# A strided-slice copy whose transfers are issued under a limit of six per queue

## The chip, the cores and the metric

The kernel runs on one core of a Trainium2 chip. The metric is device time in microseconds (us), the median over repeated executions; lower is better. The kernel does no arithmetic: it only moves data, so the engines that matter are the two that issue transfers, SyncE (SP) and ScalarE (ACT), and the core's 16 DMA engines that carry them out.

## The reference

```python
batch, seq, dim = 32, 1024, 512          # float32
start, stop, stride = 0, 512, 2
def reference(x, start, stop, stride):
    return x[:, start:stop:stride, :].astype(np.float32)
```

Of each of the 32 batches every second row among the first 512 is kept: 256 rows of 512 floats, 2 KB each. The output has the shape (32, 256, 512), which is 16.78 MB, so 16.78 MB must be read from HBM and 16.78 MB written to it.

## The kernel before

Each batch's 256 kept rows are split by the parity of their place into two halves of 128 rows. `two(t, b, step, parity)` (line 16 and on) picks one such half of the two batches `b` and `b + step`: 128 x 2 rows of 2 KB, 512 KB. `apart(b)` says which parity of batch `b` goes which way. Every transfer in the kernel has this form, 256 pieces of 2 KB.

One half goes straight from HBM to HBM: 16 transfers, issued by ACT on line 40. The other half goes through on-chip memory: 16 loads into the tile `held`, issued by SP on line 39, and 16 stores out of it, issued on line 47, eight by SP and eight by ACT. So each of the two queues gets 24 transfers of 512 KB, and 25.17 MB are moved in all, since half of the data is moved twice. Below, the transfers of a queue are numbered from #0 to #23 in the order of their issue: SP's #0 to #15 are loads and #16 to #23 stores; ACT's #0 to #15 are direct copies and #16 to #23 stores.

The order is written out by hand, inside a section that the framework does not reorder. The first loop (lines 35 to 40) alternates a load on SP and a direct copy on ACT, for four groups of eight batches. The second loop (lines 41 to 47) goes over the groups again: both engines wait until the group's four loads have landed (lines 42 and 43, one semaphore `loaded` per group, 64 counts), and then issue the group's stores, SP for even and ACT for odd `b`. `held` has room for all batches, so no transfer waits for a buffer. At the end SP waits for all stores of its own and for everything that ACT issued (lines 48 and 49, the semaphores `done`). An engine issues its transfers in this order, each instruction behind the one before it; nothing in the code says how many transfers may be under way.

Of the kernel before, what the change touches and what calls it, by code (L numbers as in the profile page):

```python
# [3 lines left out]

EIGHT = 8


def apart(b):


    return 1 - (b >> 1 & 1)


def two(t, b, step, parity):

    return t[b : b + step + 1 : step].rearrange("b (p two) d -> two p b d", two=2)[parity]


def kernel(tc, x, start, stop, stride, out):

    nc = tc.nc
    src = x[:, start:stop:stride, :]
    B, rows, D = out.shape
    P = rows // 2
    sp, act = nc.sync, nc.scalar
    groups = range(0, B, EIGHT)
    with tc.tile_pool(name="io", bufs=1) as io:  # L30
        held = io.tile([P, B, D], x.dtype, name="held")
        with tc.tile_critical():
            loaded = [nc.alloc_semaphore(name=f"loaded{g}") for g in groups]
            done = [nc.alloc_semaphore(name=f"done{i}") for i in range(2)]
            for g in groups:
                for i, (b, step) in enumerate(((0, 5), (2, 5), (1, 3), (3, 3))):
                    b += g
                    at = g + 2 * i
                    sp.dma_start(held[:, at : at + 2], two(src, at, 1, 1 - apart(at))).then_inc(loaded[g // EIGHT], 16)
                    act.dma_start(two(out, b, step, apart(b)), two(src, b, step, apart(b))).then_inc(done[1], 16)  # L40
            for g in groups:
                for queue in (sp, act):
                    queue.wait_ge(loaded[g // EIGHT], 16 * 4)
                for b in range(g, g + 4):
                    k = b % 2
                    to = two(out, b, 4, 1 - apart(b))
                    (sp, act)[k].dma_start(to, held[:, b : b + 5 : 4]).then_inc(done[k], 16)
            sp.wait_ge(done[0], 16 * (B // 4))
            sp.wait_ge(done[1], 16 * (B // 2 + B // 4))


# [1 line left out]
_INS = ['x', 'start', 'stop', 'stride']  # L53
_OUTS = [((32, 256, 512), 'float32')]

_NUMBERS = {'start': 0, 'stop': 512, 'stride': 2}


def kernel(**inputs):
    import numpy as _np  # L60
    import concourse.bacc as _bacc
    import concourse.tile as _tile
    from concourse import mybir as _mybir
    from concourse.bass_utils import run_bass_kernel_spmd as _run

    nc = _bacc.Bacc("TRN2", target_bir_lowering=False, num_devices=1)  # L66
    arrays, args = {}, []
    for name in _INS:
        if name in _NUMBERS:
            args.append(_NUMBERS[name])  # L70
            continue
        a = _np.ascontiguousarray(inputs[name])
        if a.dtype.kind in "iu":
            a = a.astype(_np.int64)
        arrays[f"in_{name}_dram"] = a
        args.append(nc.dram_tensor(f"in_{name}_dram", a.shape, _mybir.dt.from_np(a.dtype), kind="ExternalInput").ap())
    for i, (shape, dtype) in enumerate(_OUTS):
        dt = _mybir.dt.from_np(_np.dtype(dtype))
        args.append(nc.dram_tensor(f"out_{i}_dram", shape, dt, kind="ExternalOutput").ap())
    with _tile.TileContext(nc) as tc:  # L80
        kernel(tc, *args)
    r = _run(nc, [arrays], core_ids=[0])
    got = tuple(r.results[0][f"out_{i}_dram"] for i in range(len(_OUTS)))
    return got[0]
```

## Time and profile before

| | |
|---|---|
| median of 5 runs | 81.22 us (81.00 to 82.00) |
| profiled execution, its own time | 82.17 us |
| span of its instructions | 80.4 us |
| outside the span | 1.8 us |
| moved by the DMA engines | 25.17 MB, mean 313 GB/s over the span |
| transfers, KB each, per queue | 24 of 512 KB on SP's queue, 24 on ACT's |
| median from issue to landing | 22.6 us (direct copies), 22.9 us (loads), 21.6 and 21.0 us (stores) |

No compute engine does anything but four tiny fills at the start. In the profile's table of slices, a digit is the mean busy share of the 16 DMA engines in tenths in one fortieth of the span (2.01 us), and the row under it is what they moved in GB/s. The two queues are named q1 and q10 there. An issue of a transfer is an instruction on SP or ACT (shown as SPq and ACTq); its duration is the time for which it holds its engine, not the time of the transfer. "To landing" is the time from the start of the issue to the last of the transfer's sixteen semaphore counts. In the profile's account by windows, the DMA share is the same busy share over a chosen stretch; as overlaps are counted, it can read slightly over 1. A "wait" of SPq is the time for which the engine stood at a semaphore.

### The profile page before, as it was taken

The numbers are of one execution on the slowest core, as the hardware profiler recorded it, in microseconds if no ns is written. First come the engines' busy times: TensorE is split into PE (matmuls) and PEld (weight loads), VectorE is DVE, ScalarE is ACT, GpSimd is POOL, SyncE is SP. The second block draws the span as 40 slices with busy tenths as digits, with TensorE's granted clock in tenths as the row PEclk, the third lists the DMA queues.
The fourth block names the chain that finished last, engine by engine and source line by source line (L and its number), as shares of the span: only waits on it lengthen the run. The fifth ranks groups of instructions, "written<-read, shape, count | busy, mean of one in ns | idle before, by whom it ended". The sixth has DMA issues, their size and how long they took to land. (4 is left out here: it accounts for less than half of the span.)

```text
span 80.4 us, 99 instructions
## 1 busy us (share of the span) xinstructions
POOL 0.2 (0%) x4
## 2 busy tenths in 40 slices
POOL 0000000000000000000000000000000000000000
DMA  0897699999999999999999999999999999999920
GB/s 0 267 306 214 175 328 378 373 334 373 357 281 400 378 305 314 302 295 224 356 374 348 350 367 324 319 335 408 409 406 367 349 347 352 356 353 360 342 94 8
DMA packets 13056, 25.17 MB, mean 313 GB/s; under 512 B 768, under 2 KB 768, under 8 KB 13056
## 3 DMA queue, kind: packets, MB, share of 16 engines
q1 hardware_dynamic: 6528, 12.58, 47.4%
q10 hardware_dynamic: 6528, 12.58, 46.9%
HBM read 16.78 MB, written 16.78 MB: 417 GB/s over the span
## 5 line engine op out<-in xcount | busy, mean ns | idle before, releaser
L66 POOL MEMSET const-bfloat16-1.0<- 128x1 bf16 x1 | 0.1, 101 | 0.0
L66 POOL MEMSET const-uint8-127<- 128x1 uint8 x1 | 0.1, 101 | 0.0
L66 POOL MEMSET const-float32-0.0<- 128x1 f32 x1 | 0.1, 98 | 0.2 <-issue 0.2
L66 POOL MEMSET const-float32-1.0<- 128x1 f32 x1 | 0.1, 98 | 0.0
## 6 DMA issues: line engine op xcount, KB each, us to landing
out_dram<-in_x_dram ACTq DMA_DIRECT2D x16, 512.0 KB, 22.6
held<-in_x_dram SPq DMA_DIRECT2D x16, 512.0 KB, 22.9
out_dram<-held SPq DMA_DIRECT2D x8, 512.0 KB, 21.6
out_dram<-held ACTq DMA_DIRECT2D x8, 512.0 KB, 21.0
```

Source lines behind the costliest of these rows:

```text
L66: nc = _bacc.Bacc("TRN2", target_bir_lowering=False, num_devices=1)
```

## The change

A helper class `Paced` takes the place of the plain issues, one object per queue. It numbers the queue's transfers, gives each two in a row a semaphore of their own (32 counts when both have landed), and before it issues the first of a new pair from the fourth pair on, it makes the issuing engine wait until the pair three before it has landed in full. So with #6 the engine waits for #0 and #1, with #8 for #2 and #3, and so on; at most six transfers of a queue are under way, and four just before a pair is issued. The transfers, their order on each queue, their shapes and what they move stay as they are. The waits for a group's loads become waits for two pairs (line 63 of the new kernel), and the final wait of SP goes over 16 semaphores (lines 66 to 68) where it was two.

```diff
+class Paced:
+    def __init__(self, nc, engine, name):
+        self.nc, self.engine, self.name = nc, engine, name
+        self.sems, self.n = [], 0
+
+    def start(self, to, frm):
+        if self.n % 2 == 0:
+            self.sems.append(self.nc.alloc_semaphore(name=f"{self.name}{self.n}"))
+            if len(self.sems) > 3:
+                self.engine.wait_ge(self.sems[-4], 32)
+        self.engine.dma_start(to, frm).then_inc(self.sems[-1], 16)
+        self.n += 1
+
+    def wait(self, on, first, last):
+        for sem in on.sems[first // 2 : last // 2]:
+            self.engine.wait_ge(sem, 32)
...
-            loaded = [nc.alloc_semaphore(name=f"loaded{g}") for g in groups]
-            done = [nc.alloc_semaphore(name=f"done{i}") for i in range(2)]
+            sp, act = Paced(nc, nc.sync, "sp"), Paced(nc, nc.scalar, "act")
...
-                    sp.dma_start(held[:, at : at + 2], two(src, at, 1, 1 - apart(at))).then_inc(loaded[g // EIGHT], 16)
-                    act.dma_start(two(out, b, step, apart(b)), two(src, b, step, apart(b))).then_inc(done[1], 16)
+                    sp.start(held[:, at : at + 2], two(src, at, 1, 1 - apart(at)))
+                    act.start(two(out, b, step, apart(b)), two(src, b, step, apart(b)))
             for g in groups:
                 for queue in (sp, act):
-                    queue.wait_ge(loaded[g // EIGHT], 16 * 4)
+                    queue.wait(sp, g // 2, g // 2 + 4)
                 for b in range(g, g + 4):
-                    k = b % 2
-                    to = two(out, b, 4, 1 - apart(b))
-                    (sp, act)[k].dma_start(to, held[:, b : b + 5 : 4]).then_inc(done[k], 16)
-            sp.wait_ge(done[0], 16 * (B // 4))
-            sp.wait_ge(done[1], 16 * (B // 2 + B // 4))
+                    (sp, act)[b % 2].start(two(out, b, 4, 1 - apart(b)), held[:, b : b + 5 : 4])
+            for queue in (sp, act):
+                sp.wait(queue, B // 2, queue.n)
+            sp.wait(act, 0, B // 2)
```

More of the change, by code (lines that the diff above doesn't have):

```diff
@@ L27 @@
     P = rows // 2
-    sp, act = nc.sync, nc.scalar
     groups = range(0, B, EIGHT)
```

## The prediction

> **What bounds the kernel now.** I read the slices of the page first, then the account by windows, then the issues in order of time, then SP's waits. The slices and the queues:
>
> ```profile
> DMA  0897699999999999999999999999999999999920
> GB/s 0 267 306 214 175 328 378 373 334 373 357 281 400 378 305 314 302 295 224 356 374 348 350 367 324 319 335 408 409 406 367 349 347 352 356 353 360 342 94 8
> q1 hardware_dynamic: 6528, 12.58, 47.4%
> q10 hardware_dynamic: 6528, 12.58, 46.9%
> ```
>
> The DMA engines are busy nearly throughout, 94.3% of 16 engines' span, so the time is set by how fast they move 25.17 MB. Two places are not at 9: the start (slices 2 to 6) and the tail (the last two). And a slice at 9 can still be slow: 281 and 224 GB/s are at 9 too; there the engines are busy but their packets take longer. I then cut the span where the rate changes. Columns are: stretch, its length, POOL's busy time, granted clock, DMA share, GB/s.
>
> ```profile
> 4.00:6.00 2.00, 0.00 (x0) 1.00 0.96 307
> 6.00:7.00 1.00, 0.00 (x0) 1.00 0.95 279
> 7.00:9.50 2.50, 0.00 (x0) 1.00 0.53 151
> 9.50:12.00 2.50, 0.00 (x0) 1.00 1.01 309
> 12.00:22.00 10.00, 0.00 (x0) 1.00 1.05 364
> ...
> 24.00:36.00 12.00, 0.00 (x0) 1.00 1.03 331
> 36.00:38.40 2.40, 0.00 (x0) 1.00 1.01 243
> 38.40:54.00 15.60, 0.00 (x0) 1.00 1.03 346
> 54.00:62.00 8.00, 0.00 (x0) 1.00 1.05 399
> 62.00:76.00 14.00, 0.00 (x0) 1.00 1.05 352
> ```
>
> The reader is to see one row: from 7.0 to 9.5 us the share is 0.53, that is, half of the engines stand idle, though by 7.0 us 14 transfers have been issued, two more are being issued and only one has landed. Everywhere later the share is about 1. So the only idle DMA time of any size between ramp and tail is here. What do the issuing engines do then?
>
> ```profile
> 5.98 2.43 SPq L39 DMA_DIRECT2D held<-in_x_dram  x1
> 6.75 6.66 ACTq L40 DMA_DIRECT2D out_dram<-in_x_dram  x1
> ...
> 8.45 0.93 SPq L39 DMA_DIRECT2D held<-in_x_dram  x1
> 9.42 7.75 SPq L39 DMA_DIRECT2D held<-in_x_dram  x1
> ```
>
> Columns: start, duration. The first issues take 0.43 to 1.05 us each; ACT's #7, at 6.75 us, is held for 6.66 us, SP's #7 for 2.43 and SP's #9 for 7.75. From then on most issues take 2.2 us or more: issue is stopped by what is under way. The first such stop and the half-idle stretch begin together. That is a coincidence in time and no proof of a cause.
>
> **How many are under way without the limit.** Each queue moves 24 transfers between about 2 and 79 us, one per 3.2 us. A median landing 22.6 us after issue makes 22.6 / 3.2 = 7 under way. So the change takes a natural depth of about seven to between four and six. This is the quantity to keep in mind: the steady state is hardly touched, the start is (by 9.4 us SP has issued nine and begun a tenth, ACT has finished seven and hangs in the eighth; paced, each stops at six).
>
> **The change part by part.**
>
> *The pacing waits* (nine on each queue). Behind each wait on SP and ACT stand only later transfers of the same queue and, on SP, the final wait; so a late refill costs only if the queue runs dry. When a pair is released, four transfers are left, 4 x 3.2 = 12.8 us of work. Against it stands the refill: a wait passed, two issues of about 0.5 us, and from issue to first bytes about 1.1 us (first issue at 0.91, packets from 2.0), 2.2 us together. Engines do not land together, so the lagging one counts: in the tail the stretch 77.2 to 78.8 us runs at 47 GB/s, an eighth of the full rate, so some engines are 1.6 us behind. 12.8 - 2.2 - 1.6 leaves 9 us of cover. Price: 0. Should the cover be gone, each refill would expose up to 2.2 us, 20 us over nine.
>
> *The load waits* (line 63). #16 of either queue needs loads #0 to #3, which landed by 17.3 us; SP's #16 was issued at 34.7. The profile shows 0.5 us of waiting for loads in the whole kernel, with queues full. Later groups are as old. Price: 0.
>
> *The first stop.* If the half-idle stretch comes from issuing into a full queue, the limit removes it, since #6 to #9 are then issued after #0 to #3 have landed. Worth: in 2.5 us 151 GB/s were moved; at the 364 GB/s of the stage behind it this takes 2.5 x 151/364 = 1.04 us, so 1.46 us are gained. Bounds: nothing at one end; at the other the neighbours come up to 364 as well, 1.0 x (1 - 279/364) + 2.5 x (1 - 309/364) = 0.61 us more, 2.07 together. I take 1.46, because only that stretch has idle engines; the neighbours have busy ones. What is late next after it is the same transport, at its own rate, so the gain passes to the end in full.
>
> *The final wait.* In the built program SP ends with eight rows that only wait, most for two semaphores, and a branch with one more; the last pair of ACT, which lands last, stands in the second of the eight. So six rows and the branch follow the last landing, against the branch alone before: six rows more. Before, the wait of line 49 and the branch behind it stand at 79.185 and 79.250 us, 65 ns apart with the second satisfied: 6 x 0.065 = 0.39 us. Bounds: 6 x 17 ns, the row's own duration, 0.10 us; and 6 x 0.25 us, what SP waits per barrier with another engine (0.5 us in two), 1.5 us. I take 0.39, since it is the same engine and the same kind of row. It lies on the path: nothing runs beside it.
>
> ```profile
> SPq L49 <- DMA out_dram<-held: 19.4, 1, 19.4
> ...
> SPq L80 <- PEq L80: 0.5, 2, 0.3
> ```
>
> SP's 19.4 us at line 49 are the drain of what was issued by 59.7 us. Paced, the last issue comes later and this wait gets shorter, at no gain.
>
> **Sum.** The profiled execution took 82.17 us, 80.4 of it the span. 82.17 - 1.46 + 0.39 = 81.10. The median of the runs is 0.95 us under that execution, so on the median's scale: 80.15, say **80.2 us**, 1.3% less than 81.22. A caveat belongs here: if the 0.95 us by which this execution was longer lie in the very stretch that I count on, only 0.5 us are to be gained, and the sum is 81.1.
>
> One rule of the Trainium skill speaks against the gain. DMA: Bandwidth & Descriptors, section "Anatomy of one DMA — SWDGE (gpsimd) path", says that semaphore waits happen on the issuing sequencer and that "the SDMA engines just consume their queues". By it an engine with transfers queued is at work, when they were issued matters nothing, and the sum would be the second case below. The row from 7.0 to 9.5 us differs: a share of 0.53 with 13 transfers issued and not landed at its start.
>
> **The rivals.**
>
> *A, the forecast: the idle stretch goes.* For it: the stretch begins when issue first stalls, and no stall of issue would be left. Against it: later issues stall as long (6.73 us from 36.00) with a share of 1.01, so a full queue by itself does not idle engines. 80.2 us, from 79.2 (2.07 gained, 0.10 paid) to 81.1.
>
> *B, the change does not do what it is there for.* The depth was near six already, the pause at the start has another cause (the ramp, or a memory stall that hits half of the engines) and stays. Then only the longer final wait is left: 81.22 + 0.39 = 81.6 us, up to 82.7 at the upper bound of that wait.
>
> *C, slower: refills in bursts.* Each released pair is two issues at once. Before, two quick-then-long issues in a row came four times after the first burst: SP at 8.45 and 9.42, ACT at 13.44 and 14.11, SP at 34.72 and 36.00, ACT at 38.95 and 39.92. Two of the four lie at a dip, the one at 7.0 to 9.5 and the one at 36.0 to 38.4, 243 GB/s against 331 in the stage ahead: 2.4 x (1 - 243/331) = 0.64 us. Paced, there are nine such moments, both queues at nearly the same time. If half of them, four, have a dip, 2.56 us are lost; with the early pause gone (-1.46) and the final wait (+0.39) the time is 81.22 + 1.49 = 82.7 us. Two dips (1.28) cancel A's gain of 1.07; from three on (+0.85) it is slower by 1%. All nine would give 85.9. Against it: the other two of the four have no dip, and the 54 to 62 us stretch, with issues in it, is the fastest of all.
>
> **How the numbers follow.** A 0.42, B 0.31, C 0.27. Under 1% (0.8 us) a measurement of this kernel can hardly tell from none. Of A, 0.37 are faster by over 1% and 0.05 within it; of B 0.28 within and 0.03 slower; of C 0.24 slower and 0.03 within. Faster 0.37, same 0.36, slower 0.27. The range goes from A's lower end, 79.2, to 83.0, just over C's 82.7 and B's upper end; C with five dips or more is left out. A's own range is 79.2 to 81.1.
>
> **What the profile after would show.** A: slices 4 and 5 near 300 or more with a digit of 9, no issue over 1.1 us, long waits at the limit's semaphores in place of long issues, and 0.4 us from the last landing to the branch. B: the same pause at 7 us with six issued per queue. C: slices near 220 to 280 GB/s that come once per pair, about every 6.4 us. I am wrong in the cover if the share falls under 0.9 in the middle, each time before a refill; and in the size if the median kernel never had the whole pause that its one profile shows.

## The result and the profile after

| | before | paced |
|---|---|---|
| median | 81.41 us (90 runs) | 81.81 us (50 runs) |
| profiled execution, its own time | 82.17 us | 82.58 us |
| span | 80.4 us | 80.8 us |

The ratio is 1.0052, with a 95% interval of 1.0038 to 1.0065: 0.4 us slower, a small loss but clear of the noise of so many runs. Both profiled executions took about 0.8 us more than the median of their kernel, so the two are compared with each other and not with the medians. The forecast was 80.2 us, 1.3% faster. The second rival, "only the longer final wait is left", had said 0.39 us slower.

First the slices of the paced kernel, as for before: the busy share of the 16 DMA engines in tenths, and what they moved.

```profile
DMA  0899998999999999999999999999999999999920
GB/s 0 264 314 248 304 225 268 388 353 357 349 345 363 340 351 300 187 325 343 356 377 347 351 335 351 269 335 406 409 402 351 348 348 349 352 357 351 348 99 0
q1 hardware_dynamic: 6528, 12.58, 48.1%
q10 hardware_dynamic: 6528, 12.58, 47.2%
```

The change did what it says, and half of the sign that I had named for the forecast came true: no slice of the start falls under 8, where before the fourth and fifth were at 7 and 6. Of their rates, which were to be near 300 or more, one is 304 and the other 248. The time did not fall. The row of rates shows what came instead. Before, the low slices of the start were 214 and 175 GB/s at 6 to 10 us. Here they are 225 and 268 GB/s at 10 to 14 us: a like loss, two slices later. By windows (length, POOL, clock, DMA share, GB/s), the paced kernel:

```profile
7.00:9.50 2.50, 0.00 (x0) 1.00 0.89 274
9.50:10.60 1.10, 0.00 (x0) 1.00 1.01 294
10.60:13.00 2.40, 0.00 (x0) 1.00 1.07 210
13.00:14.00 1.00, 0.00 (x0) 1.00 0.95 309
...
6.00:14.00 8.00, 0.00 (x0) 1.00 1.00 261
14.00:54.00 40.00, 0.00 (x0) 1.00 1.02 335
54.00:62.00 8.00, 0.00 (x0) 1.00 1.05 396
62.00:76.00 14.00, 0.00 (x0) 1.00 1.06 351
```

The stretch from 7.0 to 9.5 us, 151 GB/s before, now moves 274. Then 10.6 to 13.0 us moves 210. In the trace's packet records eight packets of ACT's queue, which normally take 84 ns, begin between 10.66 and 11.05 us and all end within 0.06 us of 13.0; the longest took 2.36 us. The records do not name the engine of a packet; by the number of packets, about half of the engines stand still again, this time with a packet open, which counts as busy. A busy share cannot tell a working engine from one that waits in the middle of a packet; the rate can. Over 6 to 14 us the rate was 273 GB/s before and is 261 now, and the three later rows agree with the kernel before (335, 399 and 352) within 1%.

SP's waits in the paced kernel (what for, total, times, longest) show where the limit took hold:

```profile
SPq L32 <- DMA held<-in_x_dram: 26.6, 5, 6.1
SPq L38 <- DMA out_dram<-held: 16.8, 1, 16.8
SPq L31 <- DMA held<-in_x_dram: 15.6, 3, 6.0
SPq L31 <- DMA out_dram<-held: 4.6, 1, 4.6
```

The nine refills of SP wait 26.6 + 15.6 + 4.6 = 46.8 us in all (five on the issue itself, four on the row ahead of it), where before the issues were held for up to 7.75 us each. The longest issue is now 1.0 us. The median from issue to landing fell from 22.9 to 16.1 us for loads and from 22.6 to 16.5 us for direct copies. None of it shows in what was moved: from 2 to 54 us it was 322 GB/s before and 320 paced.

What is on the path stands at the end. By the trace's records the last transfer lands at 79.17 us before and at 79.21 us paced, practically the same. The branch behind the final wait stands at 79.25 before, 0.08 us after that landing, and at 79.65 paced, 0.44 us after it.

### The profile page after: what moved, and what is told of

Same layout as the page of the kernel before. It is cut to its first block, busy times and chain, and to the rows that moved or that the text cites. A ratio compares the mean times of both kernels' runs of the same rounds, so it can differ in the third digit from the quotient of the medians.

```text
span 80.8 us, 114 instructions
## 1 busy us (share of the span) xinstructions
POOL 0.2 (0%) x4
## 2 busy tenths in 40 slices
DMA packets 13056, 25.17 MB, mean 312 GB/s; under 512 B 768, under 2 KB 768, under 8 KB 13056
## 6 DMA issues: line engine op xcount, KB each, us to landing
out_dram<-in_x_dram ACTq DMA_DIRECT2D x16, 512.0 KB, 16.5
held<-in_x_dram SPq DMA_DIRECT2D x16, 512.0 KB, 16.1
out_dram<-held SPq DMA_DIRECT2D x8, 512.0 KB, 16.5
out_dram<-held ACTq DMA_DIRECT2D x8, 512.0 KB, 16.1
```

## The experiments

**Is the loss the final wait, or the limit?** Two kernels cross the two parts of the change. The first keeps the limit and shortens the final wait: pairs that the limit's own waits have covered are not waited for again, and ACT's last pair, the last to land, stands on the branch.

```diff
+            sp.wait(act, act.n - 2, act.n)
             for queue in (sp, act):
-                sp.wait(queue, B // 2, queue.n)
-            sp.wait(act, 0, B // 2)
+                sp.wait(queue, queue.n - 6, queue.n - 2)
+            sp.wait(sp, sp.n - 2, sp.n)
```

> The paced kernel with its final wait cut from sixteen semaphores to the six that the limit's own waits have not covered, with ACT's last pair on the branch itself. After the last landing only the branch is left, as in the kernel before, instead of six rows and the branch. If the whole loss of 0.4 us is the final wait (wait theory): ratio to before 1.000 (0.998 to 1.002), about 0.4 us under the changed kernel. If the limit itself costs the time (limit theory): ratio still 1.005.

Measured: 0.9966 (0.9932 to 0.9999), 81.09 us. The second has no limit, but a final wait as long as that of the paced kernel:

```diff
+            met = [(sem, n) for n in (16, 32, 48, 64) for sem in loaded]
+            last = [(done[0], 16 * (B // 4)), (done[1], 16 * (B // 2 + B // 4))]
+            for sem, n in met[:6] + last + met[6:14]:
+                sp.wait_ge(sem, n)
-            sp.wait_ge(done[0], 16 * (B // 4))
-            sp.wait_ge(done[1], 16 * (B // 2 + B // 4))
```

> The kernel before, unpaced, with fourteen more waits at its end, all long satisfied, so placed that six rows and the branch follow ACT's last landing, as in the paced kernel. Wait theory: 6 x 0.065 = 0.39 us longer, ratio 1.005. Limit theory: ratio 1.000, since nothing is paced.

Measured: 1.0058 (1.0026 to 1.0091), 81.81 us. The long final wait alone makes the loss, without any limit; and without it the limit loses nothing. From the last landing to the branch the records show 0.08 us before, 0.44 paced, 0.02 in the first of these kernels and 0.43 in the second. The rows of the final wait by source line (duration in ns as minimum, median, maximum; first and last start), in the kernel before, whose second semaphore is waited for by the branch itself:

```profile
L49 SPq EVENT_SEMAPHORE  x1: 17/17/17, 79.2 to 79.2; - x1
```

In the paced kernel:

```profile
L38 SPq EVENT_SEMAPHORE  x8: 17/28/16762, 62.4 to 79.6; - x8
```

In the paced kernel with the short wait:

```profile
L38 SPq EVENT_SEMAPHORE  x3: 17/28/28, 67.4 to 78.0; - x3
```

In the unpaced kernel with the long wait:

```profile
L51 SPq EVENT_SEMAPHORE  x8: 17/28/19454, 59.3 to 79.1; - x8
```

The last three have eight rows, three rows and eight rows. Where there are eight, one of them really waits, for 16.8 and 19.5 us; the last six are met already and follow each other 59 to 67 ns apart in the records, though a row itself lasts 28 ns. The three rows of the short wait all start ahead of the last landing, which came at 78.15 us.

**Does the limit bring anything by itself?** The 0.9966 left room for a gain of up to 0.7%. So the short wait was run again, beside a kernel with the same semaphores but no limit, and one with a limit of four. The final wait of each names the pairs that its own limit has not covered, with ACT's last pair on the branch:

```diff
-            if len(self.sems) > 3:
-                self.engine.wait_ge(self.sems[-4], 32)
+            if len(self.sems) > 2:      # limit of four; 12 for none, 1 for a limit of two
+                self.engine.wait_ge(self.sems[-3], 32)
```

> The paced kernel with the short final wait once more, beside the next two. The first time it stood at 0.9966 (0.9932 to 0.9999) to before. If the limit itself brings a little (limit gain theory), again about 0.997; if it brings nothing (neutral theory), 1.000.

> One semaphore per two transfers and the short final wait, but no limit: the pacing waits are gone, the issue runs into the full queue as in the kernel before. It is the control for the semaphores. Neutral theory: 1.000, the same as the run beside it. Limit gain theory: 1.000 here and 0.997 there. If splitting the semaphores is what gains: 0.997 in both.

> The limit at four transfers of a queue in place of six, short final wait. By the prediction's working of the cover, two transfers are left at a refill, 2 x 3.2 = 6.4 us, against 2.2 us for the refill and 1.6 us of lag: 2.6 us are left, so no price: 0.997 to 1.002. If the cover is thinner than that working says (thin cover theory): a few per cent slower, 1.02 to 1.05.

| kernel, all with the short final wait | ratio to before | 95% interval |
|---|---|---|
| limit of six, again | 1.0005 | 0.9982 to 1.0027 |
| no limit | 1.0013 | 0.9988 to 1.0037 |
| limit of four | 0.9992 | 0.9968 to 1.0015 |

The three cannot be told from each other or from before. The gain that the first run hinted at did not come again, so the neutral theory holds: between four transfers and about seven, how many are under way makes no difference here that these intervals could show.

The kernel without a limit tells one thing more. It waits for all 24 semaphores at its end, in twelve rows, more than any of the others; but all twelve start ahead of the last landing, and the branch follows that landing after 0.02 us. So it is not the number of rows that costs time here but how many stand behind the last landing.

**What is the cover worth?** With a limit of two a queue is empty at each of its refills.

> The limit at two transfers, short final wait: at each of eleven refills the queue is empty. By the prediction's working each exposes up to 2.2 us, and the 1.6 us of lag besides, in which the other queue may or may not fill in. Cover theory: clearly slower, between 11 x 1 = 11 us and 11 x 3.8 = 42 us, 1.13 to 1.5, and a share that falls under 0.8 before each refill. If a drained queue costs nothing because the other one fills the engines: under 1.05.

Measured: 1.068 (1.0636 to 1.0724), 5.5 us slower. So depth does matter at two, but the measured ratio lies between the two forecasts, above 1.05 and below 1.13. Each queue has eleven refills, so 5.5 us is 0.5 us for each pair of them, one on SP and one on ACT, where I had reckoned with 1 us at the least. Two windows of its trace, from an execution of 87.66 us, show where the share falls lowest:

```profile
9.25:11.25 2.00, 0.00 (x0) 1.00 0.27 78
40.50:43.75 3.25, 0.00 (x0) 1.00 0.33 125
```

A share of 0.27 and 0.33: here one queue has no packet open for most of the time and the other is down to the last pieces of its pair, two to four packets at once in the records (in the first window SP's refill is issued at 9.65 us, ACT's only at 10.81). At most other refills the other queue still has a pair under way, and the pause is shorter. That this help is why the price came out lower is argued from the trace and was not tested.

**Does a full queue cause the half-idle stretch?** The forecast's gain rested on this. The kernel before was profiled once more, and its first six loads and first six direct copies were run alone, where nothing is refilled, one execution of each:

```diff
+                    if issued == 6:
+                        break
+                    issued += 1
...
-            for g in groups:
-                for queue in (sp, act):
...
+            sp.wait_ge(loaded, 16 * issued)
+            sp.wait_ge(done, 16 * issued)
```

> The kernel before, unchanged, for a second profile. If issuing into a full queue idles half of the DMA engines (the mechanism of the forecast, called issue theory), the half-idle stretch is here again: a DMA share of about 0.5 for 2 to 2.5 us, beginning when the first issue is held, at 6 to 7 us. If it is a stall on the side of the memory that hits eight engines now and then (memory theory), it may be shorter, gone or elsewhere, and stalls of eight engines that end together are to be found at other times.

> Only the first six loads and the first six direct copies, issued as before, and nothing after them: the remaining loads, all stores and the remaining direct copies are left out. No queue is ever full and no refill takes place. Issue theory: no stretch with half of the engines idle, and no group of eight packets held together, from 7 us until the transfers run out, at about 12 x 0.524 MB / 0.36 MB per us = 17.5 us after the first bytes, so at about 20 us. Memory theory: a stall of about eight engines for about 2 us still comes somewhere between 6 and 16 us.

The first six alone, by windows:

```profile
4.00:6.00 2.00, 0.00 (x0) 1.00 1.02 318
6.00:7.00 1.00, 0.00 (x0) 1.00 0.89 266
7.00:9.50 2.50, 0.00 (x0) 1.00 0.51 180
9.50:12.00 2.50, 0.00 (x0) 1.00 1.02 328
```

The share is 0.51 from 7.0 to 9.5 us, where it was 0.53 in the kernel before, with SP done issuing at 5.08 us and ACT at 5.90. No issue was held: the longest took 1.01 us. The theory of the full queue falls with this one row. The paced kernel issues these same twelve transfers and nothing else up to its first refill at 9.64 us, and its share in this stretch was 0.89: with the same issues, one execution has the pause there and another does not. The second profile of the kernel before has a shorter pause, 6.5 to 8.25 us by the packet records, and the one with the long final wait, also unpaced, has no half-idle stretch there, but eight packets of ACT's queue held together from 17.45 to 19.66 us:

```profile
6.00:7.00 1.00, 0.00 (x0) 1.00 0.95 246
7.00:9.50 2.50, 0.00 (x0) 1.00 0.96 275
17.40:19.70 2.30, 0.00 (x0) 1.00 1.04 253
```

The same profile has a half-idle stretch later on, with a share of 0.46 and 164 GB/s from 33.4 to 34.8 us. So the pause is not fixed to a point of the program: it comes often near 7 us and also elsewhere, changes from one execution to the next, and groups of held packets come with a limit or without. In the four paced profiles with a limit of six or four the half-idle form lasts 0.4 us at most; in three of the four unpaced ones it lasts 1.4 to 2.5 us. If the limit changes the form, which so few executions do not show, it does not change the rate: over 6 to 14 us the four unpaced profiles moved 273, 294, 293 and 302 GB/s (mean 290) and the four paced ones 261, 280, 294 and 286 (mean 280), and over 2 to 54 us they moved 322, 323, 318 and 325 against 320, 323, 323 and 324. All eight are slower from 6 to 14 us than from 14 to 54 us (326 to 336 GB/s), so the start has a part in it that no run here explains.

**Which transfers have it?** The direct copies and the loads were run alone, and the first six once more, one execution of each.

> ACT's sixteen direct copies alone, issued without a limit; loads and stores are left out. If the stalls of about eight engines for 1.5 to 2.5 us belong to the copies from HBM to HBM (direct theory): at least one such group of packets or half-idle stretch is in this profile. If they need loads and direct copies side by side (mixture theory): none here and none in the run of the loads alone. Time by the rate of the mixed stage: 8.39 MB at 0.36 MB per us, 23 us of data, span about 27 us.

> SP's sixteen loads alone, issued without a limit; direct copies and stores are left out. Direct theory: no stall of eight engines, a share near 1 throughout, and a rate at or over the 0.36 MB per us of the mixed stage. If loads have the pause as well (start theory: something of the first microseconds that hits half of the engines whatever they do): a share of about 0.5 for about 2 us between 6 and 10 us.

> The first six loads and direct copies alone, a second time (the rest of the work is left out as in the first). If the pause at 7 us comes at every start: a share of about 0.5 between 7.0 and 9.5 us again. If it comes now and then: another place, another length, or none, as in the profiles of the full kernels, where it was seen at 7.0 to 9.5 and 6.5 to 8.25 us and once not at all.

The direct copies alone, 31.5 us of span, have it twice: half idle from 10.0 to 10.75 us with eight packets held at once behind it, and eight packets that end together at 22.35 us.

```profile
9.90:10.75 0.85, 0.00 (x0) 1.00 0.55 200
10.75:11.65 0.90, 0.00 (x0) 1.00 1.02 232
19.00:20.00 1.00, 0.00 (x0) 1.00 1.03 391
20.00:22.35 2.35, 0.00 (x0) 1.00 1.02 208
```

The loads alone have a shorter stop, fifteen packets of 0.29 to 0.76 us that end between 4.92 and 5.32 us, and a share of 0.78 to 0.85 from 6 to 12 us without such a group. The first six alone, the second time, are half idle only from 7.0 to 7.5 us, and then six packets of ACT's queue are held until 9.12 us; from 7.0 to 9.5 us the share is 0.91 and the rate 215 GB/s, against 0.51 and 180 the first time. So in a kernel cut to its first transfers the slow stretch comes at the same place, in another form. The mixture theory falls, for a single queue is enough. The direct theory fits most of the long groups, whose packets were mainly those of ACT's direct copies, but not strictly, since the loads alone had a stop too and a share that was not near 1. What holds half of the engines at once, and whether the idle form and the held packets are one thing, is not settled by these runs; they rule out that it needs a full queue, refills or both kinds of transfer, no more.

## Why the prediction was wrong

**What failed: the first stop, 1.46 us of gain, which came out at nothing** (the limit of six with the short final wait: 0.9966 and 1.0005 of before; no limit beside the second: 1.0013). The step read "If the half-idle stretch comes from issuing into a full queue, the limit removes it". The condition is false: the stretch is there at the same place with six transfers per queue and nothing held (share 0.51). I had written that the coincidence of the first held issue and the pause was no proof, and that later issues were held as long with the share at 1.01; I gave the case 0.42 all the same. That second observation was the better evidence: the supposed cause occurred many times, and the effect once. The other half of the step, "so the gain passes to the end in full", failed too: in the paced profile the pause at 7 us is gone and another one, from 10.6 to 13.0 us, has taken its place.

**The caveat, and where the time of an execution lies.** I had written that the 0.95 us by which the profiled execution lay over the median may lie in that pause. The two profiles of that kernel speak against it. The second profile of the same kernel, with the shorter pause, took 81.05 us, 1.1 us less. But the two had moved the same by 76 us, for what was left to move is the same within 0.01 MB (the first profile, then the second):

```profile
76.00:80.40 4.40, 0.00 (x0) 1.00 0.21 73
76.00:80.40 4.40, 0.00 (x0) 1.00 0.22 74
```

By the packet records the execution with the long pause was 0.16 MB behind at 14 us and level at 62 us, with 19.91 MB in both. The 1.1 us come at the very end: the last landing is at 79.17 us in the one and at 78.04 us in the other, with the same amount of data left at 76 us. So in this pair the time lost in the pause was made up later, and the gain of its removal could not pass to the end; how it was made up no run shows. A single profile shows one draw of what changes from run to run, and I priced that draw as if every run had it and as if the rest of the run stayed as it was.

**What held.** The final wait: worked out 0.39 us, measured 0.44 - 0.08 = 0.36 us in the records and 0.4 us between the medians. The row spacing, 65 ns, was read from one pair of rows and came out at 59 to 67 ns. It is the whole result. The cover: 9 us of it at a limit of six, price 0; the limit of four, with 2.6 us by the same working, was free as well. The natural depth of about seven: a limit of six hardly touches the steady state, 335 GB/s from 14 to 54 us in both. The load waits cost nothing.

**The rivals.** B was what happened, in size too (81.6 forecast, 81.81 measured with before at 81.41), though which of the two causes it offered for the pause is right stays open: the ramp alone is not it, since a pause of that kind also comes at 17, 20 and 33 us, and a stall on the side of the memory was not tested by itself. C, dips at each refill, did not happen: groups of at least four packets that take over 0.6 us and end together are seen 2 to 5 times in the four unpaced profiles and 1 to 7 times in the four paced ones, fewer than nine in each, and the last two intervals of a limit of six and of four leave a cost of 0.3% at most. C's pairing of dips with quick issues was weak too: the stretch from 7.0 us began 1.4 us ahead of the quick issue at 8.45. The upper bound of the exposed refill, 2.2 us each, was too high: with a limit of two the loss was 0.5 us for a refill of both queues together.

**The rule that I weighed.** The sentence of the Trainium skill (DMA: Bandwidth & Descriptors, "Anatomy of one DMA — SWDGE (gpsimd) path") that the DMA engines just consume their queues gave the right sum, against my reading of the row. That section describes transfers issued by GpSimd, and here SP and ACT issue; I carried it over. The runs do not settle whether it holds to the letter: half of the engines were idle with at least 10 of 12 transfers issued and not landed, and the trace does not show whether those engines had pieces in their queues just then. But holding back the issue brought no time, and this is what the rule was used for.

## What to carry to other kernels

Where the engines that move the data are supplied throughout, as here, expect that pacing the issue moves waiting from one instruction to another and brings nothing; count the transfers under way (landing time over time per transfer) before building it, and check what each additional semaphore adds behind the last landing. A final wait should leave as few rows as possible after the event that lands last: put that event on the last instruction and leave out what other waits have covered. And a pause that is seen once in one profile is to be looked for in a second profile, and in a kernel cut down to its first transfers, before its removal is entered into a sum.

## What the runs showed of the hardware that was not expected

- About eight of the 16 DMA engines stop together for 0.9 to 2.5 us and go on together; their number is read from the share and from the count of packets. It shows as a half-idle stretch (share 0.51 and 0.53) or as up to eight packets, 84 ns long as a rule, that take up to 2.4 us and end within 0.1 us of each other, and it comes in another place from execution to execution. It was seen while loads or direct copies were under way, and in no profile after 59 us with a limit of four or more or none, when only stores are left.
- A wait on a semaphore that has long been reached is not free: where several rows of waits follow each other, each row, most with two semaphores, takes 59 to 67 ns of SP's time.
- The end of the kernel has two speeds in each of the eight full profiles without a limit or with one of four or six: 392 to 399 GB/s from 54 to 62 us and 348 to 352 GB/s from 62 to 76 us, when only stores are left. Why was not tried.
- The last landing comes between 78.04 and 79.21 us in these eight profiles, with 24.66 to 24.94 of the 25.17 MB moved by 76 us in each, and the two profiles of the kernel before, level at 24.84 MB then, land 1.1 us apart: the last pieces alone differ by that much from execution to execution.
